# Softmax rows of the first block's attention scaled on DVE in place of POOL

## The chip, the cores and the metric

One core of a Trainium2 chip (trn2) runs the kernel. The metric is the device time of one execution in microseconds (us), the median of several runs; lower is better. The engines of the core run side by side, each through its own fixed list of instructions, in order, and wait for one another by semaphores: TensorE (PE) multiplies matrices, VectorE (DVE) and ScalarE (ACT) work element by element, GpSimd (POOL) does that too, SyncE (SP) issues DMAs.

## The reference

Two transformer blocks over a sequence of 1024 tokens with 1024 channels, in f32. The first block has three kinds of attention side by side, four heads each: latent attention with a chunk mask (MLA), causal attention with a forget gate (Fox), and attention to a band of chunks with a relative bias. Then come an output projection, cross attention and a gated feed-forward layer. The second block follows behind. What matters here is the softmax of the first block's heads:

```python
sc = jnp.einsum('bqhd,bkhd->bhqk', qb, k, preferred_element_type=jnp.float32) * scale
sc = jnp.where(k_chunk[None, :] <= q_chunk[:, None], sc, -jnp.inf)
p = jax.nn.softmax(sc, axis=-1).astype(v.dtype)
return jnp.einsum('bhqk,bkhd->bqhd', p, v)
```

Each row of `p` is the exponentials divided by their sum, before it is multiplied with the values.

## The kernel before

All of it is one program on one core. Matrices are kept as two f32r halves, high and low, and a product is three matmuls (`mm3`, lines 380, 387 and 388). The halves are made by `split` (lines 352 and 353: ACT copies the high half, DVE subtracts it for the low one); of the weights by lines 282 (ACT) and 283 (DVE).

The attention of the first block goes over 12 heads: 0 to 3 MLA, 4 to 7 Fox, 8 to 11 banded. Each head has 8 row tiles of 128 queries, so there are 96 row tiles. Row tile b has K = 128 (b + 1) keys in the first two kinds, at most 640 in the third. `heads_attend` (line 811) hands them to `g_attend` (line 733), a software pipeline written out by hand. Each of its steps emits, in this order: the scaling of the row tile whose exponentials were made a step before (`softmax_scale`); the split of the transposed probabilities; the exponentials of the last row tile (`softmax_exp`, line 723, ACT, which also makes the sums); the scores of the next one (PE) and its maxima (`softmax_max`, lines 707 to 714, DVE); the transposes of up to four blocks of scaled probabilities (line 786, PE); the multiplication with the values (line 801, PE). The tiles `p` are 1024 columns wide and there are 5 of them.

Into this, `weave` (line 1175 calls it) puts fill work for PE: the cross attention's keys and values and the output projections of finished kinds of heads (`g_wo`, whose sums are added by line 1016 on DVE). The inputs of a coming head are prepared inside the pipeline too; for heads 4 to 11 that is `prep64`, with memsets on POOL (lines 1038 and 1041), a subtraction of one row on POOL (line 1062, heads 4 to 7), and subtractions on DVE (lines 1048, 1051 and 1053). `fold` (line 861, DVE) adds the two halves of an output. `power` (line 452) is a small operation on POOL for a norm.

The order on each engine isn't the emitted one alone: the kernel is built with a planner that simulates the program (`schedule_with_timeline_sim=True`, line 2348) and puts the instructions of each engine in order by that and by priorities. The fill work has a lower priority.

The line that changes is 730, at the end of `softmax_scale`: line 728 adds the two partial sums of a row wider than 512 (DVE), line 729 takes the reciprocal (DVE), line 730 multiplies the row by it, in place. The cross attention (line 1321) and the second block's attention (line 2113) have scalings of their own, on POOL.

Of the kernel before, what the change touches and what calls it, by code (L numbers as in the profile page):

```python
# [11 lines left out]
ALU = mybir.AluOpType  # L12
# [91 lines left out]
def tile_net(ctx: ExitStack, tc: tile.TileContext, I: dict, out: bass.AP):  # L104
    nc = tc.nc
    V, A, G, T = nc.vector, nc.scalar, nc.gpsimd, nc.tensor
# [564 lines left out]
    with tc.tile_pool(name="ring", bufs=1) as ring:  # L671
        in0 = lambda f: ("in", 0)
# [53 lines left out]
    def softmax_scale(n, sm, p, K):  # L726
        if n == 2:
            V.tensor_tensor(out=sm[:, 0:1], in0=sm[:, 0:1], in1=sm[:, 1:2], op=ALU.add)
        V.reciprocal(out=sm[:, 0:1], in_=sm[:, 0:1])  # L729
        G.tensor_scalar(out=p[:, :K], in0=p[:, :K], scalar1=sm[:, 0:1], scalar2=1.0, op0=ALU.mult, op1=ALU.mult)  # L730

    def g_attend(pool, rows, scores, maxes, exps, norm, items_after, live_max, head=None, ptb=2):

# [77 lines left out]
    def heads_attend(pool, heads, scale_of, scores, items_of, out_of, prep, late, live_max=4):  # L811
# [24 lines left out]
        def head(row, before):  # L836
# [12 lines left out]
            if bg[1] is not None:  # L849
                next(bg[1], None)  # L850
                next(bg[1], None)

        return g_attend(pool, [(h, b) for h in heads for b in range(8)], g_scores, maxes, exps,
                        lambda row, st: softmax_scale(*st), items_after, live_max, head)

    def fold(dst, ps, odd, w):
# [564 lines left out]
    with tc.tile_pool(name="ff", bufs=1) as ff:  # L1421
# [271 lines left out]
        for (so, gname, gi) in ((8, "norm_g_2", 0), (32, "norm_g_2", 8), (56, "kv_norm_g_2", 0)):  # L1693
            V.scalar_tensor_tensor(out=ada[:, so:so + 8], in0=ada[:, so:so + 8], scalar=1.0, in1=vc(gname, gi, 8),
                                   op0=ALU.add, op1=ALU.mult)
# [656 lines left out]
```

## Time and profile before

| what | us |
|---|---|
| median of 3 runs | 2468.51 (2468.14 to 2470.2) |
| profiled execution | 2466.64 |
| its span, first to last instruction | 2464.9 |
| PE busy | 2351.1 (95%) |
| DVE busy | 1813.4 (74%) |
| ACT busy | 1115.7 (45%) |
| POOL busy | 575.5 (23%) |
| line 730, all 96 | 81.7, the first at 224.7, the last at 558.2 |

How to read it: busy time is the union of the engine's instructions in one profiled execution; matmuls overlap one another, so a busy PE need not be at its peak. PEclk is the share of TensorE's full clock that was granted. An average over the span hides stages with other limits, so the rows below are mostly of the stretch in which line 730 runs.

### The profile page before, as it was taken

The page shows a single profiled execution, that of the slowest core. Times are in us where ns is not written, and L with a number is a line of the kernel's source. Part 1 is how long each engine was busy: PE and PEld are TensorE (multiplying, and loading weights), DVE is VectorE, ACT ScalarE, POOL GpSimd, SP SyncE. Part 2 cuts the span into 40 slices and gives each one's busy share as a digit, 9 for nine tenths or more (in the row PEclk, how much of TensorE's full clock was granted, in tenths as well). Part 3 has the DMA queues.
Part 4 walks back from the last instruction along what each step waited for, and adds up shares of the span by engine and source line. Part 5 has one row for each costly group of instructions (what it writes and reads, how often), then busy time and mean ns, then how long its engine had stood idle before and what let it go on. Part 6 is the DMA issues. An engine that isn't in the chain of part 4 may idle for free.

```text
span 2464.9 us, 33653 instructions
## 1 busy us (share of the span) xinstructions
PE 2351.1 (95%) x11534; PEld 1927.5 (78%) x11534; DVE 1813.4 (74%) x3427; ACT 1115.7 (45%) x2325; POOL 575.5 (23%) x555
## 2 busy tenths in 40 slices
PE   8999989898999999999999979999999997999997
PEld 6888977777877778888888858887788885888876
DVE  6425788898669788887788797667775457788865
ACT  5224686675554333333444554333332125566652
POOL 4102254334222222221000230000000017444442
PEclk9999998999999999999999989999999998999999
DMA  5223123433241656655644414333553221111223
GB/s 165 91 80 94 57 61 102 121 116 129 67 148 51 201 184 212 193 198 175 220 149 144 150 56 162 107 105 105 188 188 112 69 78 33 48 59 59 69 82 120
DMA packets 145184, 292.48 MB, mean 119 GB/s; under 512 B 24996, under 2 KB 37780, under 8 KB 145012
## 3 DMA queue, kind: packets, MB, share of 16 engines
q1 hardware_dynamic: 145012, 290.33, 36.3%
q8 instruction: 91, 1.49, 0.3%
q14 instruction: 81, 0.66, 0.1%
HBM read 222.38 MB, written 67.86 MB: 118 GB/s over the span
## 4 chain that ended last, share of the span: by engine, by line
PE 75%; DVE 11%; DMA 4%; issue 4%; ACT 3%; POOL 2%; SPq 0%; POOLq 0%; DVEq 0%; ACTq 0%
PE wd L380 7%; PE wd L387 7%; PE wd L388 7%; PE fx L1406 6%; PE fx L1407 6%; PE fx L1408 6%; PE fz L1408 3%; PE fz L1406 3%; PE fz L1407 3%; PE mm L380 2%; PE mm L387 2%; PE mm L388 2%; PE tp L786 2%; PE op L801 2%; DMA araw<-in_ada_w 2%
## 5 line engine op out<-in xcount | busy, mean ns | idle before, releaser
L1407 PE MATMUL fx<-R,wl 128*128 128x512 f32 x736 | 291.9, 397 | 3.6 <-DVE wl L267 3.6
L1406 PE MATMUL fx<-R,wh 128*128 128x512 f32 x736 | 289.1, 397 | 2.6 <-ACT ev L1843 2.4
L1408 PE MATMUL fx<-R,wh 128*128 128x512 f32 x736 | 289.4, 396 | 1.3 <-DVE R L353 1.3
L282 ACT ACTIVATE wh<-wraw 128x1024 fp32r<-128x1024 f32 (+2 forms) x124 | 124.3, 1004 | 245.3 <-PE wd L388 180.7
L452 POOL TENSOR_TENSOR nr<-nv,half 128x4 f32<-128x4 f32 (+1 forms) x25 | 26.0, 1043 | 660.5 <-DVE nv L446 653.6
L1407 PEld LDWEIGHTS fx<-R,wl 128*128 128x128 f32 x736 | 138.3, 188 | 38.6 <-DVE wl L267 5.6
L1406 PEld LDWEIGHTS fx<-R,wh 128*128 128x128 f32 x736 | 138.4, 188 | 37.9 <-ACT ev L1843 3.7
L1408 PEld LDWEIGHTS fx<-R,wh 128*128 128x128 f32 x736 | 138.1, 188 | 34.9 <-DVE R L353 1.6
L283 DVE TENSOR_TENSOR wl<-wraw,wh 128x1024 fp32r<-128x1024 f32 (+1 forms) x89 | 112.6, 1268 | 67.9 <-ACT wh L282 66.8
L266 ACT ACTIVATE wh<-ws 128x512 fp32r<-128x512 f32 (+1 forms) x196 | 112.0, 598 | 104.1 <-PE fx L1408 57.5
L267 DVE TENSOR_TENSOR wl<-ws,wh 128x512 fp32r<-128x512 f32 (+1 forms) x196 | 132.9, 696 | 30.5 <-ACT wh L266 30.4
L1407 PE MATMUL fz<-R,wl 128*128 128x512 f32 x368 | 146.4, 398 | 6.2 <-DVE wl L267 6.2
L1406 PE MATMUL fz<-R,wh 128*128 128x512 f32 x368 | 146.8, 399 | 4.8 <-ACT R L352 3.8
L1408 PE MATMUL fz<-R,wh 128*128 128x512 f32 x368 | 146.0, 398 | 2.7 <-DVE R L353 2.7
L353 DVE TENSOR_TENSOR ptl<-tp,pth 128x512 fp32r<-128x512 f32 (+2 forms) x196 | 123.2, 635 | 20.4 <-ACT pth L352 17.0
L730 POOL TENSOR_SCALAR p<-p,ssum 128x640 f32<-128x640 f32 (+4 forms) x96 | 81.7, 854 | 209.0 <-DVE ssum L729 141.8
L786 PE MATMUL tp<-ident,p 128*128 128x128 f32 x712 | 117.4, 278 | 11.7 <-DVE ptl L353 5.9
L1215 DVE SCALAR_TENSOR_TENSOR x<-wd,ada,x 128x512 f32<-128x512 f32 x80 | 59.9, 750 | 91.2 <-PE wd L388 91.1
L1465 DVE SCALAR_TENSOR_TENSOR aacc<-araw,cact,aacc 128x512 f32<-128x512 f32 x112 | 92.6, 827 | 39.0 <-DMA araw<-in_ada_w 38.4
L352 ACT ACTIVATE pth<-tp 128x512 fp32r<-128x512 f32 (+2 forms) x196 | 107.0, 559 | 29.7 <-PE op L801 14.9
L266 ACT ACTIVATE wh<-wraw 128x512 fp32r<-128x512 f32 (+1 forms) x98 | 58.0, 598 | 126.1 <-PE fz L1408 81.8
L786 PEld LDWEIGHTS tp<-ident,p 128*128 128x128 f32 x712 | 85.3, 142 | 24.5 <-POOL p L730 6.1
(397 smaller groups left out, 7005.6 us busy)
## 6 DMA issues: line engine op xcount, KB each, us to landing
araw<-in_ada_w SPq DMA_DIRECT2D x128, 256.0 KB, 3.4
hr<-d_h SPq DMA_DIRECT2D x63, 256.0 KB, 3.6
x<-d_x SPq DMA_DIRECT2D x48, 256.0 KB, 5.3
wraw<-in_w_gu SPq DMA_DIRECT2D x23, 512.0 KB, 4.3
sraw<-in_w_gu SPq DMA_DIRECT2D x21, 512.0 KB, 3.8
wraw<-in_a_w_in SPq DMA_DIRECT2D x20, 512.0 KB, 3.8
wraw<-in_a_w_out SPq DMA_DIRECT2D x20, 512.0 KB, 3.6
d_h<-H SPq DMA_DIRECT2D x36, 256.0 KB, 2.2
```

Of the source, the lines that this page charges most:

```text
L266: A.activation(out=wh, in_=raw, func=AF.Copy)
L267: V.tensor_tensor(out=wl, in0=raw, in1=wh.bitcast(F32), op=ALU.subtract)
L282: A.activation(out=wh[:, sl], in_=raw[:, sl], func=AF.Copy)
L283: (G if pool_split[0] else V).tensor_tensor(out=wl[:, sl], in0=raw[:, sl], in1=wh[:, sl].bitcast(F32), op=ALU.subtract)
L353: V.tensor_tensor(out=l, in0=src, in1=h.bitcast(F32), op=ALU.subtract)
L380: ins = T.matmul(ps, lhsT=wh, rhs=xh, start=start, stop=False)
L387: T.matmul(ps, lhsT=wl, rhs=xh, start=False, stop=False)
L388: T.matmul(ps, lhsT=wh, rhs=xl, start=False, stop=stop)
L786: T.transpose(tp[:, (o + j) * 128:(o + j + 1) * 128], b, ident)
L1406: T.matmul(ps, lhsT=wh[:, sl], rhs=rh[k], start=new and k == 0, stop=False, skip_group_check=not new)
L1407: T.matmul(ps, lhsT=wl[:, sl], rhs=rh[k], start=False, stop=False, skip_group_check=not new)
L1408: T.matmul(ps, lhsT=wh[:, sl], rhs=rl[k], start=False, stop=k == nk - 1, skip_group_check=not new)
```

## The change

In `softmax_scale` the multiplication of the row by the reciprocal of its sum moves from POOL (`G`) to DVE (`V`), behind the reciprocal, and its second factor of 1.0 is dropped. Nothing else is edited; the planner orders the instructions anew.

```diff
         V.reciprocal(out=sm[:, 0:1], in_=sm[:, 0:1])
-        G.tensor_scalar(out=p[:, :K], in0=p[:, :K], scalar1=sm[:, 0:1], scalar2=1.0, op0=ALU.mult, op1=ALU.mult)
+        V.tensor_scalar(out=p[:, :K], in0=p[:, :K], scalar1=sm[:, 0:1], scalar2=None, op0=ALU.mult)
```

## Rows read from the trace of the kernel before

**Rows 1.** The page's first part: busy us (share of the span) xinstructions of each engine.
```profile
PE 2351.1 (95%) x11534; PEld 1927.5 (78%) x11534; DVE 1813.4 (74%) x3427; ACT 1115.7 (45%) x2325; POOL 575.5 (23%) x555
```

**Rows 2.** Stretches of the first block's attention, busy us (xinstructions) by engine.
```profile
core 0: us, PE busy (x) PEld busy (x) DVE busy (x) ACT busy (x) POOL busy (x), PEclk, DMA share, GB/s
222.00:300.00 78.00, 77.77 (x572) 70.71 (x571) 59.01 (x133) 46.62 (x113) 20.66 (x23) 0.99 0.22 65
300.00:340.00 40.00, 38.73 (x298) 35.14 (x297) 34.95 (x80) 33.04 (x77) 17.58 (x18) 1.00 0.27 81
340.00:380.00 40.00, 27.56 (x167) 23.21 (x167) 33.55 (x76) 33.19 (x72) 23.91 (x22) 0.76 0.16 40
380.00:470.00 90.00, 88.28 (x515) 74.66 (x515) 72.45 (x176) 59.36 (x133) 32.58 (x34) 0.97 0.44 129
470.00:562.00 92.00, 79.24 (x522) 66.45 (x520) 83.53 (x263) 68.03 (x176) 27.59 (x36) 0.98 0.31 95
sum 340.00, PE 311.59 PEld 270.16 DVE 283.49 ACT 240.25 POOL 122.33; mean PE 62.32 PEld 54.03 DVE 56.70 ACT 48.05 POOL 24.47
```

**Rows 3.** The same stretches, the instructions of line 730 alone.
```profile
222.00:300.00 78.00, 13.82 (x19) 0.99 0.22 65
300.00:340.00 40.00, 10.12 (x10) 1.00 0.27 81
340.00:380.00 40.00, 10.74 (x10) 0.76 0.16 40
380.00:470.00 90.00, 22.44 (x24) 0.97 0.44 129
470.00:562.00 92.00, 24.60 (x33) 0.98 0.31 95
sum 340.00, POOL 81.74; mean POOL 16.35
```

**Rows 4.** POOL's groups by line and shape, 222 to 562 us: busy us, mean ns.
```profile
L730 POOL TENSOR_SCALAR p<-p,ssum 128x640 f32<-128x640 f32 x24 | 22.7, 947 | 55.0 <-DVE ssum L729 37.6 <-ACT pth L352 7.0 <-ACT p L723 4.4
```

**Rows 5.** DVE's groups by line and shape: two from 470:562 us, one from 222:562.
```profile
L1048 DVE TENSOR_TENSOR q<-n,q 64x512 fp32r<-64x512 f32 x4 | 3.5, 888 | 0.1
L1051 DVE TENSOR_TENSOR k<-n,k 64x512 fp32r<-64x512 f32 x4 | 2.6, 687 | 0.1
...
L1051 DVE TENSOR_TENSOR k<-n,k 64x512 fp32r<-64x512 f32 x16 | 12.9, 845 | 0.2
```

**Rows 6.** The timeline around 370 us: start us, us, instruction, idle time before it.
```profile
369.40 2.93 POOL L1041 MEMSET q<- 64x1024 f32 x3
372.43 1.55 POOL L730 TENSOR_SCALAR p<-p,ssum 128x768 f32<-128x768 f32 x1
...
370.64 0.15 DVE L729 RECIPROCAL ssum<-ssum 128x1 f32<-128x1 f32 x1
...
374.03 0.47 PE L786 MATMUL tp<-ident,p 128*128 128x128 f32 x1 [4.66 <-POOL p L730]
```

**Rows 7.** Single lines 1463 and 714: duration ns min/median/max, first and last start us.
```profile
L1463 DVE TENSOR_SCALAR aacc<-araw,cact x16: 469/480/1264, 799.6 to 1131.5; 128x512 f32<-128x512 f32 x16
...
L714 DVE TENSOR_SCALAR mx<-mx x56: 187/209/215, 235.0 to 556.0; 128x1 f32<-128x1 f32 x56
```

**Rows 8.** Two DVE instructions in a row, from the timeline near 553 us.
```profile
552.82 0.55 DVE L353 TENSOR_TENSOR ptl<-tp,pth 128x384 fp32r<-128x384 f32 x1
553.29 0.40 DVE L861 TENSOR_TENSOR ya<-op,fold 64x256 f32<-64x256 f32 x1
```

**Rows 9.** The timeline near 1105 us, DVE and POOL.
```profile
1105.70 1.26 DVE L1463 TENSOR_SCALAR aacc<-araw,cact 128x512 f32<-128x512 f32 x1 [0.17 <-DMA araw<-in_ada_w]
...
1105.07 1.60 POOL L1581 TENSOR_TENSOR H<-H,c 128x512 f32<-128x512 f32 x1 [15.36 <-ACT H L1579]
```

**Rows 10.** One more stretch, columns as in Rows 2.
```profile
490.00:530.00 40.00, 37.80 (x242) 31.43 (x241) 38.41 (x123) 31.73 (x80) 12.37 (x17) 1.00 0.40 119
```

## The prediction

> **What bounds the kernel now.** I read the page's busy line first, then the table of stretches over the first block's attention, then the same table for line 730 alone, then the single rows around the scale. The busy line shows TensorE (PE) busy for 95% of the span, and DVE for 74% [rows 1]. That says only that over the whole kernel DVE has room. The scale is in the program only 96 times, from 224.7 to 558.2 us, so the stretches from 222 to 562 us are what counts, and there the picture differs [rows 2]. From 222 to 300 us PE is busy for 77.77 of 78 us: PE bounds. From 300 to 380 us PE has 66.3 of 80 us, DVE 68.5. From 380 to 470 us PE has 88.28 of 90 again. From 470 to 562 us PE has 79.24 of 92 us and DVE 83.53: DVE is the busiest engine. Over the 340 us DVE is busy for 283.5 us, so 56.5 us are free, but only 8.5 us of them lie in the last stretch. POOL has 122.3 us of 340, and 81.7 us of that are the scales [rows 2, 3]. So an engine with much room gives work to one with little, and where DVE has least room, in the 92 us of the third kind of head, the scales are densest: 33 of 96 [rows 3].
>
> **What is removed.** POOL loses 96 instructions, 81.7 us [rows 3]; that the POOL engine gets time back is worth nothing by itself. Three things come with it. First, a 640 wide scale took 947 ns there on the mean [rows 4], and the transposes of that row wait for it. Second, POOL and DVE hold each other up: the 64x512 subtraction of line 1048 took 888 ns from 470 to 562 us, where that of line 1051 with the same shape took 687, and over all heads line 1051 took 845 [rows 5]. Freed of the scales, lines 1051 and 1048 give back some 16 x 0.16 = 2.5 us and 1 us, and others of that kind perhaps as much as the latter. I take 3.5 us, of which 1 in the last stretch (4 x 0.2 for line 1048, the rest an estimate). Third, a scale no longer stands in POOL's queue behind the memsets of a head's preparation. Once that is seen on PE: the reciprocal ran at 370.64 us, POOL was busy with memsets from 369.40 until its scale began at 372.43 and took 1.55, and PE stood still for 4.66 us until 374.03 [rows 6]. What stood behind the scales in POOL's queue (those memsets, the subtraction of line 1062, the power of line 452) can only come earlier.
>
> **What is added, instruction by instruction.** The new DVE operation takes one SBUF tensor in f32 and a scalar for each partition. The trace has this kind once, line 1463: 128x512 in 480 ns, median of 16. The same kind on one column, line 714, took 209 ns, median of 56 [rows 7]. So a scale of K columns costs 209 + 0.53 (K - 1) ns: 549 ns at 640, 753 at 1024. Eight heads have rows of 128 to 1024 columns, four have 128, 256, 384, 512 and four of 640: 52,224 columns in all, 96 x 0.209 + 52.1 x 0.53 = 47.7 us. On a full DVE the next operation begins before the last one's end: 0.55 us from 552.82 us, the next at 553.29 [rows 8], so 0.08 us less each, 7.7 in all. The addition is 40.0 us: 12.3 for the 32 rows of the third kind of head, and 27.7 shared out over the other stretches by POOL's time in them [rows 3]: 6.7, 4.9, 5.2 and 10.9.
>
> The scale can in turn be held up by what POOL still does, 122.3 - 81.7 = 40.6 us, 3.0 of them in the last stretch [rows 2, 3]. Line 1463 was held up once: 1.26 us against 0.48, while a POOL operation that began before it ran until 1106.67 [rows 9]. If each POOL operation that is left held up a scale whenever they meet, 40.6 / 340 x 96 = 11 scales would lose up to 0.8 us each. I take 3 us, between 0 and 9; nearly all of it from 300 to 470 us, where the heads with memsets are prepared.
>
> What is queued behind the scale on DVE, as the code emits it: the low half of the transposed probabilities (line 353), on which PE's multiplication with the values waits, and the row maxima (line 710), on which the exponentials and then PE's score buffers wait. Both come up to 0.55 us later for each row where DVE has no idle time, and nobody notices where it has. No DMA and nothing in SP's queue is moved.
>
> **The sum, stretch by stretch.** How full can DVE be in this work? From 490 to 530 us it was busy for 38.41 of 40 us, 96% [rows 10]. I take that share as the limit; 100% and the stretch's present share are the ends. From 470 to 562 us: 83.53 + 12.3 - 1 + 0.3 = 95.1 us of DVE in 92 us; at 96% that is 99.1, so +7 (at 100% +3, at the present 91% +12.7). From 300 to 340 us: 34.95 + 4.9 - 0.7 + 1 = 40.2; at 96% 41.8, so +2 (0 to +6). From 340 to 380 us: 33.55 + 5.2 - 0.7 + 1 = 39.1, at 96% 40.7, +0.7; but the stall at 374 us shortens: the reciprocal ended at 370.79, a 768 wide scale ends 0.62 us later at 371.4, and POOL's ended at 373.98, which is 2.6 us earlier [rows 6]. DVE was itself full there, so I count 1.7 of it: -1 (-4 to +4). From 380 to 470 us: 72.45 + 10.9 - 1 + 1 = 83.4 of 90, 93%: covered by 17.5 us of idle DVE time, 0 (0 to +2). From 222 to 300 us: 59 + 6.7 of 78: covered by PE's own work, 0. The sum is +8 us (7 + 2 - 1), with ends of about 0 and +20. What comes behind 562 us can't give it back: the output projection needs the last rows of the last head.
>
> The order of instructions on each engine is set by a planner when the kernel is built, which may place other work around the scales; that is why I take 96% and not the present share.
>
> The profiled execution took 2466.64 us, 1.7 more than its span, and the median of the runs is 1.9 above it. Put on the median: 2468.5 + 8 = 2476.5.
>
> **A rule against the row.** A rule speaks against this change: the Trainium skill, "SBUF — State Buffer", section "Who interferes with whom", says that a DVE tensor_scalar in a two-port mode and a GpSimd operation exclude each other fully, whoever starts first. The trace agrees with it in one case [rows 9]; no row shows a memset doing so. By the rule the memsets would hold up scales too, which is rival (d).
>
> **The rivals.** (a) Hidden: the planner moves DVE's other work (the fill matmuls' weights and sums, the preparation of heads) into the 56.5 us of free DVE time, of which 40 are needed. For it: over the 340 us DVE would be at 94% only. Against it: the last stretch has 8.5 us free for 12.3. Time 2465 to 2473, about 2469. (b) Faster: the rows, not DVE's throughput, set the pace where PE idles. Then the stall of 4.66 us goes, and in the last stretch each hold-up that ended (1 us) and the shorter way from reciprocal to transposes (947 - 549 = 0.4 us for a 640 wide row, on PE's path once for each of four heads, 1.6 us) count: -4.7 - 1 - 1.6 = -7, 2461. It decides in the last stretch: PE is idle for 12.8 us there, and if these are waits for single rows while DVE's queue is short, this wins; for it DVE's added time must stay under the 8.5 us that are free. Against it: DVE at 91% there, and 96% for 40 us on end. (c) The operation takes twice as long per column, 1.06 ns: then 96 x 0.209 + 52.1 x 1.06 - 7.7 = 67.6 us are added, 20.4 of it in the last stretch, and at 96% that alone is +16 (103.2 / 0.96 - 92); the stretches from 300 to 470 us give another 13 (45.5, 42.8 and 94.7 for 40, 40 and 90). Time 2497. Line 1463 speaks against it; but its scalar was written long before, and it writes another tile than it reads. (d) What is left on POOL holds up the scales at each of the 11 meetings: 9 us in place of 3, 6 more than forecast, 2482. For it: the one case in the trace [rows 9]. Against it: the other 15 instructions of line 1463 have a median of 480 ns [rows 7].
>
> **How the numbers follow.** Forecast 0.45 (2471 to 2485), (a) 0.25, (b) 0.17, (c) 0.05, (d) 0.08. Faster and slower are counted from 0.2%, 4.9 us, about what a measurement of this kernel tells from no change. Slower: 0.40 of the forecast, (c), (d) and 0.02 of (a): 0.55. Same: 0.05 of the forecast, 0.21 of (a), 0.02 of (b): 0.28. Faster: 0.15 of (b) and 0.02 of (a): 0.17. The range 2462 to 2488 leaves out about half of (b), (c) and the upper end of (d) and of the forecast, 0.2 in all. The likeliest case by itself has 2471 to 2485.
>
> **What would show it.** Right: line 730 appears on DVE with about 550 ns for 640 columns; DVE over 95% busy from 470 to the stage's end, PE waiting longer there for the low halves of line 353; the stage ends 5 to 12 us later, and all that follows keeps its length. Wrong: a scale of 640 columns takes 0.87 us (c); DVE's idle time shrinks and the stage keeps its length (a); PE's idle time in the last stretch shrinks below 12.8 us (b); many scales at 1 us and more beside memsets (d). A stage that is shorter with DVE fuller would fell the rule that 96% is the limit.

## The result and the profile after

The median of after is 2490.44 us (2486.48 to 2493.43) where before has 2468.32 in the same series: a ratio of 1.0088, with a 95% interval from 1.0075 to 1.0100, so 18.5 to 24.7 us more. The forecast was 2476.5 and its range ended at 2488. The change makes the kernel slower, as forecast, but by 22 us and not by 8. The profiled execution took 2491.8 us, its span is 2490.0.

The first part of after's page, busy us (share of the span) xinstructions:

```profile
PE 2371.2 (95%) x11534; PEld 1943.7 (78%) x11534; DVE 1846.9 (74%) x3523; ACT 1118.0 (45%) x2325; POOL 498.3 (20%) x459
```

Against [rows 1], POOL lost 77.2 us and DVE gained 33.5. PE has the same instructions and is busy for 20.1 us more. DVE's share of the span is 74% in both: the average over the whole kernel shows nothing of what happened.

The new operation by shape, after, 222 to 580 us (busy us, mean ns):

```profile
L730 DVE TENSOR_SCALAR p<-p,ssum 128x640 f32<-128x640 f32 x24 | 14.8, 618 | 0.1
...
L730 DVE TENSOR_SCALAR p<-p,ssum 128x1024 f32<-128x1024 f32 x8 | 6.0, 745 | 0.0
...
L730 DVE TENSOR_SCALAR p<-p,ssum 128x128 f32<-128x128 f32 x12 | 3.9, 328 | 0.0
```

The formula said 549 ns for 640 columns, 753 for 1024 and 276 for 128. All 96 took 51.7 us; 47.7 by the formula, and 4.0 of hold-ups.

For the stretches I take the three kinds of heads one after the other: MLA, Fox, banded. Their bounds move with the kernel. As the kernel before I show here a kernel that differs from it in one scale of 128 columns only (e10 below), because before's own profiled execution starts its first row 2.9 us later than any other. First e10, then after, columns as in [rows 2]:

```profile
222.00:348.00 126.00, 120.42 (x881) 108.54 (x881) 98.53 (x222) 87.26 (x204) 46.35 (x47) 0.97 0.24 67
348.00:474.00 126.00, 113.45 (x672) 97.02 (x670) 103.60 (x245) 87.73 (x193) 49.78 (x50) 0.93 0.36 103
474.00:560.00 86.00, 75.46 (x489) 63.16 (x489) 77.35 (x250) 61.98 (x165) 26.20 (x35) 0.96 0.33 99
```

```profile
222.00:348.00 126.00, 120.11 (x880) 108.84 (x879) 110.81 (x253) 87.77 (x203) 19.78 (x15) 0.97 0.23 67
348.00:480.00 132.00, 116.78 (x673) 97.17 (x672) 116.56 (x282) 89.14 (x197) 17.71 (x17) 0.91 0.35 102
480.00:578.00 98.00, 87.46 (x489) 74.90 (x489) 85.97 (x278) 62.45 (x163) 3.76 (x3) 0.83 0.28 82
```

The MLA heads took 12 us more of DVE into the same 126 us. The Fox heads grew by 6 us, the banded heads by 12. In the banded heads DVE was at 90% (77.35 of 86) and is now at 88% (85.97 of 98): it did not fill up, the stretch grew. The granted clock of PE (the column after POOL) fell from 0.96 to 0.83 there. PE's busy time grew by 12.0 us with the same 489 matmuls, as much as the stretch: by these rows alone the lower clock could be the cause as well. The experiments take that up as theory C.

Where the later DVE is felt in the banded heads: the waits of PE and of ACT, after, 480 to 578 us (engine, line, waited for: us in total, times, longest):

```profile
PE tp L786 <- DVE ptl L353: 3.0, 3, 2.5
PE mm L380 <- DVE xt L1016: 2.8, 2, 2.6
PE tp L786 <- DVE p L730: 2.7, 1, 2.7
```

```profile
ACT p L723 <- DVE mx L714: 9.6, 10, 3.5
```

In before ACT's wait for the row maxima was 3.0 us in 6 times (474 to 558 us). So the exponentials wait longer for the maxima, which the code emits behind the scales on DVE. PE waits for DVE at several places, no longer mostly at one: in before 4.7 us of its waits there were for line 353. In all PE's waits for DVE grew little, from 7.6 us to 9.2.

The last view gives the place of the loss. Line 1406 first runs for the gated feed-forward layer and then for large products up to the second block. All of the first block's attention has to be through before its first matmul, so that is a better mark than the last row. The line's 736 matmuls into the tile `fx`, before, e10 and after (duration ns min/median/max, first and last start us):

```profile
L1406 PE MATMUL fx<-R,wh x736: 389/396/628, 740.0 to 1779.1; 128*128 128x512 f32 x184
```

```profile
L1406 PE MATMUL fx<-R,wh x736: 388/396/628, 739.8 to 1779.8; 128*128 128x512 f32 x184
```

```profile
L1406 PE MATMUL fx<-R,wh x736: 388/396/632, 757.7 to 1804.2; 128*128 128x512 f32 x184
```

After reaches it 17.8 us later than the mean of the other two. From the first to the last it takes 1046.5 us where before took 1039.1 and e10 1040.0: some 7 us more, in a part of the kernel where nothing was edited. So the loss has two parts, 18 us in the attention and 7 behind it (25 us between these two profiled executions, 22 between the medians).

### The profile page after: what moved, and what is told of

Its sections match the earlier page's. It is cut to its first block, busy times and chain, and to the rows that moved or that the text cites. A ratio compares the mean times of both kernels' runs of the same rounds, so it can differ in the third digit from the quotient of the medians.

```text
span 2490.0 us, 33449 instructions
## 1 busy us (share of the span) xinstructions
PE 2371.2 (95%) x11534; PEld 1943.7 (78%) x11534; DVE 1846.9 (74%) x3523; ACT 1118.0 (45%) x2325; POOL 498.3 (20%) x459
## 4 chain that ended last, share of the span: by engine, by line
PE 75%; DVE 13%; DMA 3%; issue 3%; ACT 3%; POOL 2%; SPq 0%; DVEq 0%; POOLq 0%; ACTq 0%
PE wd L380 7%; PE wd L387 7%; PE wd L388 7%; PE fx L1406 6%; PE fx L1407 6%; PE fx L1408 6%; PE fz L1408 3%; PE fz L1406 3%; PE fz L1407 3%; PE mm L380 3%; PE mm L387 3%; PE mm L388 2%; PE tp L786 2%; PE op L801 2%; DMA araw<-in_ada_w 2%
## 5 line engine op out<-in xcount | busy, mean ns | idle before, releaser
L353 DVE TENSOR_TENSOR ptl<-tp,pth 128x512 fp32r<-128x512 f32 (+2 forms) x196 | 123.1, 635 | 21.1 <-ACT pth L352 18.0
L786 PE MATMUL tp<-ident,p 128*128 128x128 f32 x712 | 124.2, 287 | 12.2 <-DVE p L730 7.4
L786 PEld LDWEIGHTS tp<-ident,p 128*128 128x128 f32 x712 | 89.1, 147 | 24.7 <-DVE p L730 6.0
L380 PE MATMUL wd<-Y,wh 128*128 128x512 f32 x256 | 101.2, 395 | 0.5 <-DVE sz L1914 0.5
```

The source lines that it names most:

```text
L353: V.tensor_tensor(out=l, in0=src, in1=h.bitcast(F32), op=ALU.subtract)
L380: ins = T.matmul(ps, lhsT=wh, rhs=xh, start=start, stop=False)
L786: T.transpose(tp[:, (o + j) * 128:(o + j + 1) * 128], b, ident)
```

## The experiments

Three theories stood against one another. A: DVE's time in the attention is what costs. B: what costs is the new order that the planner makes of the instructions. C: the stalls let PE's clock fall, and the low clock makes the loss.

The table puts the marks of all kernels side by side; it is worked out from their traces. "DVE" is DVE's busy time from the first to the last reciprocal of line 729, less that of before (279.3 us). "Late" is the first start of line 1406 less 739.9 (the mean of before and e10). "Clock" is the clock that PE lost between the first of these reciprocals and that start: the time, times what the granted clock lacks of 1. "150" is the time from the first to the 151st of the 736 matmuls.

| kernel | DVE, us more | late, us | clock, us | 150, us | median us | ratio (95% interval) |
|---|---|---|---|---|---|---|
| before | 0 | 0.1 | 17.1 | 222.6 | 2468.3 | 1 |
| e10, one short row | 0 | -0.1 | 16.8 | 223.5 | 2468.36 | 1.0000 (0.9987 to 1.0013) |
| e11, head 9 | 3.7 | -0.4 | 15.4 | 223.4 | 2470.47 | 1.0002 (0.9992 to 1.0011) |
| e5, heads 4 to 7 | 10.5 | -2.4 | 18.6 | 223.5 | 2473.12 | 1.0022 (1.0012 to 1.0033) |
| e6, wide rows | 21.0 | 9.1 | 21.1 | 223.3 | 2481.73 | 1.0059 (1.0044 to 1.0074) |
| e1, heads 8 to 11 | 9.5 | 6.6 | 22.1 | 228.1 | 2482.00 | 1.0062 (1.0047 to 1.0077) |
| e3, two columns | 9.9 | 4.2 | 25.6 | 228.2 | 2473.83 | 1.0031 (1.0021 to 1.0040) |
| e2, heads 0 to 7 | 24.4 | 7.7 | 26.3 | 226.6 | 2483.05 | 1.0066 (1.0049 to 1.0084) |
| e7, subtractions on POOL | -20.3 | 11.4 | 25.8 | 227.4 | 2481.97 | 1.0060 (1.0045 to 1.0075) |
| e8, after and e7's edit | 28.3 | 20.3 | 25.3 | 227.3 | 2490.42 | 1.0096 (1.0077 to 1.0115) |
| after | 33.9 | 17.8 | 32.4 | 228.6 | 2490.44 | 1.0088 (1.0075 to 1.0100) |
| e12, two factors | 34.7 | 17.6 | 28.0 | 229.1 | 2489.64 | 1.0094 (1.0077 to 1.0111) |
| e4, scale on both | 41.7 | 23.4 | 26.3 | 226.7 | 2494.80 | 1.0113 (1.0096 to 1.0130) |
| e9, twice on DVE | 71.4 | 46.1 | 37.3 | 227.6 | 2517.02 | 1.0184 (1.0160 to 1.0208) |

The profiled execution of e5 (2464.12 us) is the lowest of its ten runs, some 9 us under its median, so its row is a lower bound of what that kernel loses; the mark too strays by some us.

### One part of the heads each: e1 and e2

```diff
-        G.tensor_scalar(out=p[:, :K], in0=p[:, :K], scalar1=sm[:, 0:1], scalar2=1.0, op0=ALU.mult, op1=ALU.mult)
+        (V if h >= 8 else G).tensor_scalar(out=p[:, :K], in0=p[:, :K], scalar1=sm[:, 0:1],
+            scalar2=None if h >= 8 else 1.0, op0=ALU.mult, **({} if h >= 8 else {"op1": ALU.mult}))
```

> The scale runs on DVE in heads 8 to 11 alone, on POOL in heads 0 to 7. The changed kernel took 22 us more than before; its trace has +4 us at the reciprocal of row 61, +20 at that of row 96, +25 at the end of the span. Theory A (DVE's time in the third kind of head is what costs): +14 to +18 at row 96, and 2484 to 2491 us in all. Theory B (the loss comes with the planner's new order in the whole stage): about a third of it, +5 to +8 at row 96, 2474 to 2481 us. Theory C (a stall of PE lets its clock fall and the low clock makes the loss): +10 to +20, but with at least 10 us of lost clock in heads 8 to 11, as in the changed kernel (17 us there against 2 before).

The same with `h < 8` is e2:

> The other half: on DVE in heads 0 to 7, on POOL in heads 8 to 11. PE's order is that of the changed kernel but for the instructions of heads 8 to 11. Theory A: +1 to +5 at row 96 against before, and 2468 to 2478 us in all, the upper end if the later part, whose order is that of the changed kernel, keeps its 5 us. Theory B: most of the loss stays, +12 to +20 at row 96, 2484 to 2490 us.

The banded heads alone reach line 1406 6.6 us late, the other eight 7.7 us. The prediction had put +7 on the banded heads and about +1 on the rest: the first half was sized well, the second was not. Together they make 14.3 of after's 17.8; the last 3.5 come only with both. What theory A said of how the loss is shared out fell: it had 14 to 18 us at e1's last row and 1 to 5 at e2's, and they came 5.5 and 7.1 us later than before's. B's 5 to 8 us fit e1, but its 12 to 20 for e2 fell. C wanted at least 10 us of lost clock in e1's banded heads; 5.1 were lost, and these heads still took 8.1 us more (92.2 us from their first reciprocal to the last, 84.1 in the mean of before and e10).

### Almost none of the columns: e3

```diff
-        G.tensor_scalar(out=p[:, :K], in0=p[:, :K], scalar1=sm[:, 0:1], scalar2=1.0, op0=ALU.mult, op1=ALU.mult)
+        V.tensor_scalar(out=p[:, 0:2], in0=p[:, 0:2], scalar1=sm[:, 0:1], scalar2=None, op0=ALU.mult)
```

> On DVE in all heads, but over 2 columns of each row only; the other columns stay unscaled, so the rows' sums are not divided out. The instruction, its place behind the reciprocal and its waits stay, its time falls from 52 us in all to 96 x 0.21 = 20 us (7 in place of 17 in heads 8 to 11). Theory A: +2 to +7 at row 96, 2470 to 2480 us. Theory B: +15 to +20 at row 96, 2484 to 2490 us. If the scale's dependence on DVE were what costs (not its columns), as B.

With 96 scales of two columns DVE has 9.9 us more, and line 1406 is 4.2 us late. The step from the reciprocal through DVE to the transposes is there as in after; the columns are not. So it is not the move as such that costs 18 us: A's 2470 to 2480 us held and B's 2484 to 2490 fell. Nor is it a new order of the attention as such: on DVE, e3 and e5 have another order there than before too, and e3 is 4.2 us late, e5 not at all. Its median is 7.7 us above that of before in its series, so nearly half of that comes behind the mark, where e3 has the order of after; its 150 matmuls take 228.2 us.

### DVE's time without the dependence: e4

```diff
+        V.tensor_scalar(out=scr[0][:, :min(K, 512)], in0=scr[0][:, :min(K, 512)], scalar1=sm[:, 0:1], scalar2=None, op0=ALU.mult)
```

> The scale stays on POOL as before; behind each reciprocal DVE gets one more operation of the same kind, min(K, 512) columns of a tile that nobody reads, some 41 us in all and 14 in heads 8 to 11. No row waits for it. Theory A: the loss is there without the move, +12 to +20 at row 96 and 2482 to 2492 us. If instead the rows' way through DVE is what costs (each row's scale queued in DVE's order), nearly nothing: +0 to +4, 2468 to 2474 us.

Here the scale stays on POOL, and DVE gets an operation of the same kind on a scratch tile that nobody waits for (the tile is made and filled once, ahead of the heads). It loses more than after, and with 2494.80 us more than A's 2482 to 2492. The 96 operations took 52.4 us, 41 by the formula: 23 of them ran over it by more than 0.1 us, all while POOL was at work. The stretches of e4, columns as above:

```profile
222.00:348.00 126.00, 119.60 (x872) 108.28 (x870) 108.09 (x240) 82.33 (x190) 41.60 (x43) 0.97 0.22 64
348.00:480.00 132.00, 116.71 (x664) 96.49 (x662) 118.30 (x277) 89.09 (x199) 55.98 (x54) 0.91 0.34 99
480.00:582.00 102.00, 84.69 (x513) 71.19 (x511) 95.35 (x298) 68.80 (x177) 27.04 (x35) 0.92 0.29 88
```

DVE is at 86%, 90% and 93%, after at 88% in each, and the clock in the banded heads is 0.92 where after has 0.83. The rows' way is that of before: from the end of the reciprocal to the end of the scale on POOL 1.24 us on the mean, in before 1.22. This speaks for A: DVE's time alone, with no new way for the rows, makes such a loss. It speaks against C: a larger loss with less clock lost, 26.3 us up to the mark where after lost 32.4.

### Twice the added work: e9

```diff
         V.tensor_scalar(out=p[:, :K], in0=p[:, :K], scalar1=sm[:, 0:1], scalar2=None, op0=ALU.mult)
+        V.tensor_scalar(out=scr[0][:, :min(K, 512)], in0=scr[0][:, :min(K, 512)], scalar1=sm[:, 0:1], scalar2=None, op0=ALU.mult)
```

> After, with one more scaling of min(K, 512) columns of a scratch tile on DVE behind each scale (96 more instructions, some 41 us of DVE). Theory A (DVE's time in the stage is what costs): the first 52 us cost 22 us, and there is less idle DVE time left now, so the second 41 us cost nearly their whole length: the stage grows by 22 + 30 to 41 against before, time 2520 to 2532. Theory C (the low clock that the stalls bring made the loss): the added work shifts the stalls, and the growth follows the lost clock, between 2480 and 2510.

2517.02 us: 3 us under A's forecast, 7 above C's. In the attention (columns as above):

```profile
222.00:360.00 138.00, 125.91 (x889) 112.98 (x888) 125.09 (x283) 88.98 (x207) 20.01 (x15) 0.93 0.21 61
360.00:500.00 140.00, 122.04 (x688) 102.50 (x686) 131.25 (x320) 89.65 (x196) 20.11 (x17) 0.89 0.34 100
500.00:600.00 100.00, 80.67 (x476) 65.08 (x475) 95.06 (x306) 62.33 (x162) 3.66 (x3) 0.93 0.26 77
```

From e10 to after, 33.9 us of DVE became 17.8 us of time, 0.53 of each. From after to e9 another 37.5 us of DVE became 28.4 us (786.0 less 757.6), 0.76 of each. The share of DVE from the first to the last scale is 83% in e10, 88% in after and 93% in e9. So there is no share up to which the work is free and beyond which it costs in full: the price of one more microsecond rises with the share, and DVE comes to 91 to 95% only when the stretch has already grown by much.

### Small doses: e5, e6, e11 and the null, e10

Conditions in place of `h >= 8`: `4 <= h < 8` (e5), `b >= 4` (e6), `h in (9,)` (e11), `(h, b) == (0, 0)` (e10).

> On DVE in heads 4 to 7 alone. The kernels tried so far all lost about 6 us behind the stage, between 570 and 1500 us, where nothing is edited, and all have there the changed kernel's order of instructions; this one has the order of the kernel before. Theory A with B behind the stage (DVE's time costs in the stage, the planner's new order 6 us behind it): +5 to +8 at row 96, no more behind it (within 1.5 us), 2470 to 2476 us. If the 6 us come from something else (a later start of the stages, chance), they stay: 2476 to 2482.

> On DVE for the row tiles of 640 columns and more (b of 4 and above, 48 of 96, 36,864 of the 52,224 columns, about 30 us of DVE), on POOL for the narrow ones; behind the stage the order of the kernel before. A with B behind the stage: +9 to +16 at row 96, no more behind it, 2475 to 2483 us. If the number of the instructions moved counted and not their time, half of the stage's 22: +11; if the 6 us behind the stage are not the order's, 6 more in all.

> Before, with the scale of head 9 alone (8 row tiles, 3,968 columns, some 3.7 us of DVE in the banded heads) on DVE; PE's order behind the stage is that of before. A: a few us of DVE in the stretch with the least room, stage +1.5 to +3 us; B (the new order behind the stage costs the 4 to 6 us there): behind the stage within 2 us of before's, time 2468 to 2471. If behind the stage it is 4 us or more longer, the order there isn't the reason.

> Before, with the scale of one single row tile (the first head's first, 128 columns) on DVE. Every engine's order is that of before but for that one instruction. It measures how far a profile of the same work strays: theories A and B give 2466 to 2469, the stage's length within 2 us of before's, and the part behind the stage within 2 us of before's. If the part behind the stage is 4 us or more longer than in before's profile here too, then the 4 to 7 us that most kernels show there are no effect of the change or of the new order.

e10 gives the size of what a profile strays by. Its time is that of before and its line 1406 starts within 0.2 us of before's, but from the first to the last reciprocal it has 337.2 us where before has 333.4, because before's first row came at 224.4 us and not at 221.5. My expectation of 2 us for that length fell; the start of line 1406 is the mark that holds. Head 9 alone costs nothing that can be told from no change, heads 4 to 7 about 0.2%. e6 has 36,864 of the 52,224 columns in half of the row tiles and loses 9.1 us for 21 us of DVE.

These four have the order of before on every engine from line 1406's start on, and all of them take 223.3 to 223.5 us for the 150 matmuls, before 222.6. All kernels with a new order there, e7 and e8 among them, take 226.6 to 229.1. That is B's part: 4 to 6 us. The 1 to 2 us that are left of after's 7 come later, where e6 and e11 with before's order lose 2 to 3, and were not explained. For after, e1, e2, e3, e4 and e12 the order from that start on is one and the same, whatever they do in the attention, and from the first to the last matmul of line 1406 they take 1044.6 to 1047.4 us against 1039.1 to 1042.3. Those of e3 and e12:

```profile
L1406 PE MATMUL fx<-R,wh x736: 389/396/628, 744.1 to 1789.1; 128*128 128x512 f32 x184
```

```profile
L1406 PE MATMUL fx<-R,wh x736: 389/396/632, 757.5 to 1804.9; 128*128 128x512 f32 x184
```

e3 comes to this part 13 us sooner than after and loses the same in it, so it isn't the lateness that costs. That the order does is the reading that fits all fourteen kernels; none changed that order alone, so it is shown by grouping and not by an edit.

### The dropped factor, and the clock: e12

```diff
-        V.tensor_scalar(out=p[:, :K], in0=p[:, :K], scalar1=sm[:, 0:1], scalar2=None, op0=ALU.mult)
+        V.tensor_scalar(out=p[:, :K], in0=p[:, :K], scalar1=sm[:, 0:1], scalar2=1.0, op0=ALU.mult, op1=ALU.mult)
```

> After, with the second factor of 1.0 left in the DVE operation (scalar2 = 1.0, op1 = mult); the order of every engine is that of after. It does one part of the change alone. If the second factor costs DVE nothing, a 640 wide scale takes 0.62 us on the mean as in after and the time is 2488 to 2493; if it costs a second pass, some 0.3 us more for 640 columns and by theory A 15 us more time. Theory C: the low clock of PE in the banded heads (0.83 of the stretch in after's profile) is what makes the loss there, so it must be there again, and if it is not, the banded heads are some 10 us shorter; theory A: the stage is 354 to 358 us long whatever the clock shows. The part behind the stage 1912 to 1916 us.

The second factor costs DVE nothing. 640 columns took 618 ns on the mean in both:

```profile
L730 DVE TENSOR_SCALAR p<-p,ssum 128x640 f32<-128x640 f32 x24 | 14.8, 618 | 0.1
```

As every engine's order is that of after, e12 is also a second look at after. Its banded heads:

```profile
480.00:578.00 98.00, 84.46 (x500) 71.02 (x500) 87.58 (x279) 64.08 (x165) 3.76 (x3) 0.90 0.26 79
```

The granted clock was 0.90 here and 0.83 in after. The last reciprocal came at 572.8 us, 5 us before that of after, so my 354 to 358 us for the attention (350.7 measured) and 1912 to 1916 us behind it (1917.9) both fell. Yet line 1406 starts at 757.5 us, after's at 757.7. What lies between the last reciprocal and that start, after and then e12, columns as above:

```profile
577.77:757.68 179.91, 167.36 (x840) 137.26 (x840) 130.52 (x214) 95.76 (x204) 54.40 (x58) 0.99 0.35 118
```

```profile
572.72:757.47 184.75, 172.56 (x840) 141.60 (x840) 130.14 (x213) 95.56 (x203) 54.50 (x58) 0.96 0.34 115
```

Here e12 lost 7.5 us of clock and after 1.2, and e12 took 4.8 us longer for the same work. So the equal marks don't show that lost clock is free. In this stretch PE is busy for 93% of the time, and over all the kernels it takes 179.9 to 181.5 us where 1.2 to 2.2 us of clock are lost in it, 184.7 and 185.0 where 7.5 and 8.5 are (the longest is e9's, 186.1 with 6.0). As the main cause C falls by the table: e3, e2, e8 and e4 lost nearly the same up to the mark, 25.3 to 26.3 us, and are 4.2, 7.7, 20.3 and 23.4 us late, in the order of DVE's added time. How much of after's 17.8 us is due to the 15 us of clock that it lost beyond before's is left open.

### Relieving DVE elsewhere: e7 and e8

```diff
-                V.tensor_tensor(out=q1[64:128, hs(hf)], in0=n[0:64, hs(hf)], in1=q1[0:64, hs(hf)].bitcast(F32), op=ALU.subtract)
+                G.tensor_tensor(out=q1[64:128, hs(hf)], in0=n[0:64, hs(hf)], in1=q1[0:64, hs(hf)].bitcast(F32), op=ALU.subtract)
```

Lines 1051 and 1053 in the same way; e7 is before with this, e8 is after with it.

> The scale stays on POOL; the subtractions that prepare heads 4 to 11 (lines 1048, 1051, 1053; 40 instructions, 30 us of DVE) go from DVE to POOL. Theory A: the stage gets shorter where DVE bounds, -3 to -8 at row 96, 2456 to 2466 us. If PE's own work or the rows' way bounds, 0; if the slower preparations on POOL are waited for, longer, 2470 and above.

> The changed kernel (scale on DVE in all heads) with the same 40 subtractions on POOL: DVE gets 52 us and gives 30, 22 more than before. Theory A: the loss in the stage falls from 22 to between 2 and 9 at row 96, 2468 to 2481 us. If the rows' way through DVE's queue costs, it stays at 18 or more, 2485 and above. The collisions of scales with POOL may take back some 5 us.

Here A's forecast for e7 fell. DVE has 20 us less in the attention and the kernel is slower. The 40 subtractions cost POOL far more than DVE, e7, 222 to 580 us:

```profile
L1051 POOL TENSOR_TENSOR k<-n,k 64x512 fp32r<-64x512 f32 x16 | 21.6, 1368 | 1.1 <-POOL p L730 0.7
...
L1048 POOL TENSOR_TENSOR q<-n,q 64x512 fp32r<-64x512 f32 x16 | 20.6, 1306 | 0.6
...
L1053 POOL TENSOR_TENSOR vv<-vr,vv 128x512 fp32r<-128x512 f32 x8 | 10.9, 1367 | 4.0 <-PE sc L1069 2.0 <-ACT vv L1052 1.9
```

That is 53.1 us on POOL for 30.1 us on DVE in before, in one queue with the scales. (The Trainium skill, "GPSIMD Engine Reference", section "Engine selection", puts an operation with two inputs at some twice the time it takes on VectorE; the trace agrees, 1.37 us for the 0.69 that line 1051 takes on DVE in after.) So less work on DVE isn't a gain by itself; it has to go to a place that is not in the rows' way. The scales did queue: they began 1.38 us after their reciprocals on the mean, 8.3 at most, in before 0.37 and 3.1. How the 11.4 us that e7 is late share out between these waits and those for the slower subtractions was not settled. With the subtractions on POOL, moving the scale to DVE costs 8.4 us (2490.42 less 2481.97) where it costs 22 without. A's forecast for e8, 2468 to 2481 us, fell too: of the 30 us that left DVE only 5.6 came off its busy time (28.3 against 33.9), and the 96 scales, now beside the subtractions on POOL, took 62.7 us on DVE where after's took 51.7.

No kernel of these beat before.

## Why the prediction was wrong, point by point

**What bounds.** Right in the main. DVE is the busiest engine of the banded heads in before, and about half of what was added to it came out as time. e4 shows that DVE's time alone can do it. But the sign that PE would wait longer for the low halves of line 353 didn't come: 3.0 us in after's banded heads, 5.7 in before's.

**The price of a scale.** Right: 51.7 us against 50.7 (47.7 and 3 of hold-ups). Rival (c), twice the price per column, is out. DVE's busy time in the attention grew by 33.9 us only, where I had 39.5; the time grew by more all the same, so that error hid part of the next one.

**The hold-ups.** Right in size: 4.0 us in all, 3 forecast. Five scales make it up: 640 columns in 1.48 us at 366.57 us beside memsets, 896 columns in 1.47 at 344.81, 768 in 1.63 at 374.37 and 128 in 0.85 at 414.10 beside line 1062, 640 in 1.35 at 500.93 beside a memset. Rival (d), all meetings, is out.

**The relief.** Right: lines 1048 and 1051 came down to these, after, 222 to 580 us; from 740 and 845 ns (the latter in [rows 5]), 3.5 us in all, the forecast's number.

```profile
L1048 DVE TENSOR_TENSOR q<-n,q 64x512 fp32r<-64x512 f32 x16 | 10.4, 682 | 0.8 <-ACT q L1043 0.6
L1051 DVE TENSOR_TENSOR k<-n,k 64x512 fp32r<-64x512 f32 x16 | 10.3, 685 | 0.2
```

**The stall at 374 us.** Half right. The wait behind POOL's memsets [rows 6] is gone, and in its place are two shorter ones at the scale on DVE, of 2.17 us at 368.20 and of 1.90 at 376.05. The second, on DVE, POOL and PE:

```profile
374.31 1.27 POOL L1062 TENSOR_TENSOR k<-ch,k 1x512 fp32r<-1x512 f32 x1 [4.38 <-ACT k L1061]
374.37 1.63 DVE L730 TENSOR_SCALAR p<-p,ssum 128x768 f32<-128x768 f32 x1
...
376.05 1.33 PE L786 MATMUL tp<-ident,p 128*128 128x128 f32 x5 [1.90 <-DVE p L730]
```

I had counted a gain of 1.7 us from this stall. The scale left POOL's queue, but it was still held up by POOL.

**How full DVE can be.** This is the step that failed. I took the 96% of one stretch of 40 us [rows 10] for what the whole work can reach, and so turned 12.3 us of added work into 7 in the banded heads and nearly nothing elsewhere. Measured by kinds of heads (the mean of after and e12 less that of before and e10): MLA +0.5, Fox +4.9, banded +12.5, in all 17.9 us. The best stretch of a trace is picked because it is full; the work around it has waits that don't go away when more is put on. The other end that the prediction had written beside it, the present share of 91%, gives +12.7 for the banded heads. That this number came is not shown to be more than luck: in e1, with these heads alone moved, they grew by 8.1 us at a share of 93%, near the forecast, and in after they also lost 16.7 us of PE's clock (e12 8.5, e1 5.1). The prediction's upper ends, 12.7, 6, 4 and 2, make +24.7 and not about +20, and its range ended at +19.5. The 17.9 us lie between the two sums, +8 and +24.7. The rule named in the forecast's last sentence isn't felled by a shorter stage; it falls because DVE stayed at 88 to 90% in longer ones.

**"Covered".** The same error from the other side. I put 0 on the stretch from 380 to 470 us because 17.5 us of DVE were idle there, and -1 on the one ahead of it. e2, which touches heads 0 to 7 only, is 7.7 us late. As I read it, idle time of an engine is cover only where it lies next to the added work; and here part of it is time in which DVE itself waits for ACT and PE: in before, from 380 to 470 us, 7.3 us of it at line 1016 for PE alone.

**Behind 562 us.** The sentence that all that follows keeps its length was wrong: 7 us more between the first and the last matmul of line 1406. I had spoken of the planner's order only for the attention itself. It was made anew for the whole program, and the order differs far behind the last scale.

**PE's clock.** The forecast has no term for it. Up to the mark after lost 32.4 us of clock, before 17.1; how much of that is time is open.

**The rivals.** (a) and (b) are out: DVE's idle time took only half of the work, and PE's idle time between the rows did not become a gain. The shorter way that (b) counted on didn't come: from the end of the reciprocal to the end of the scale a banded row took 1.54 us on the mean, in before 0.90, because the scale began 1.05 us after the reciprocal, where POOL had begun it after 0.18.

## What to carry to other kernels

Before an operation is moved onto an engine, work out the stretch with the engine's present busy share there as well, and keep the fullest 40 us as the best case only: the truth lay between the two here. Between a share of 83 and 88% half of each added microsecond became time, between 88 and 93% three quarters. Where a planner orders the program anew, a small edit can cost microseconds in places that it doesn't touch; find them by the time between two marks that all kernels share. And a kernel that changes one instruction only tells how far two profiles of the same work stray: here 4 us from the first to the last reciprocal, and 0.2 us at a mark behind which all the work meets.

## What the hardware showed that was not expected

A memset on POOL held a scale on DVE up for nearly its whole length. After, DVE and then POOL around 501 us:

```profile
500.33 0.68 DVE L420 TENSOR_TENSOR acc<-acc,sq 128x512 f32<-128x512 f32 x1
500.93 1.35 DVE L730 TENSOR_SCALAR p<-p,ssum 128x640 f32<-128x640 f32 x1
```

```profile
500.99 0.95 POOL L1038 MEMSET k<- 64x1024 f32 x1 [13.41 <-PE sc L1072]
```

The same shape without a neighbour took 0.55 us (464.08 us): 0.80 us more beside a memset of 0.95. The page that the prediction cited (the Trainium skill, "SBUF — State Buffer", section "Who interferes with whom") says that a DVE tensor_scalar in a two-port mode and a GpSimd operation exclude each other. The trace agrees for a memset too. The scale's row starts 0.06 us before the memset's, but the operation ahead of it on DVE ran until 501.01, so these rows don't tell which of the two was first. A subtraction of one row of 512 on POOL (line 1062, 1.27 us) did the same to the scale of 768 columns at 374.37 us, shown above: 1.63 us where the formula has 0.62.

PE's granted clock fell at a stall. It was 0.53 from 478 to 492 us, so nearly all of that stretch ran at the lower of its two levels (1.2 of 2.4 GHz), where PE had stood still for 2.48 us before 480.39 (DVE's line 353 came late), and the same 128x256 matmul of line 801 went from 0.28 us at 475.43 to 0.41 at 482.16. That looked like the cause of the loss in after's trace; over all the kernels the time follows DVE's added time and not the lost clock.
